# A hybrid decoder block on one core: three quarters of the down-projection with seven block products instead of eight

## The chip, the core and the metric

The kernel runs on one core of a Trainium2 chip. The metric is device time in microseconds (us) of one execution. TensorE (PE in the profile) multiplies matrices, VectorE (DVE), ScalarE (ACT) and GpSimd (POOL) work elementwise, and SyncE (SP) issues every DMA of this kernel from one queue, in order. Each engine executes its instructions in the order in which they stand in its program and waits on semaphores for the others.

## The reference, cut to what matters

The block has two token mixers in parallel (a Mamba-2 scan and a gated DeltaNet), merges them, and ends with a squared-ReLU MLP. The change touches the part behind the mixers:

```python
merged = jax.nn.sigmoid(gate_ssm) * y_ssm + jax.nn.sigmoid(gate_gdn) * y_gdn
x = x + g1 * rmsnorm(merged @ w_out[l], norm_mix_post[l])

h = rmsnorm(x, norm_mlp_pre[l]) * (1.0 + sc2) + sh2
y = jnp.square(jax.nn.relu(h @ w_mlp_up[l])) @ w_mlp_down[l]
x = x + g2 * rmsnorm(y, norm_mlp_post[l])
```

There are 512 tokens, a model width of 1024 and 4096 hidden units, all in float32.

## The kernel before, in words

**Precision.** Every large product is made of three matmuls on rounded operands. A float32 operand is split into a rounded high part and a low remainder: ACT casts it (`whi`, line 145), DVE subtracts (`wlo`, line 146). The helper `mm3` (lines 150 to 152) then issues high times high, low times high, high times low. The third matmul is the one that needs the weight's low half. `dense_w` (lines 140 to 147) loads a 512 KB weight tile into `raw` (three buffers), and splits it into `whi` and `wlo` (three buffers each).

**Stages around the change.** After the mixers come the two up-projections of the branches (lines 1240 to 1267), the output projection `w_out` (lines 1333 to 1350), the norms and the residual, and the MLP. The output projection works in two halves of 256 tokens; each half uses eight weight tiles, one for every 12 matmuls. Behind each half follows a chain of small steps (`sums`, `norms`, `chans`), which ends in the transposed input `h2` of the MLP. The rows that gate and scale the residual (`gates`, built from `adr` and from `rows` through the tiles `rb`) and the residual `x1` are asked for ahead of this stage in the code (lines 1272 to 1285). A scheduler of the tile framework settles the order on each queue, so that in the program the loads of `gate` and `x1` lie in the up-projections, and the four loads of `rb` between weight tiles of the output projection.

**The MLP.** It is cut into four quarters of 1024 hidden units. A quarter has eight hidden tiles (24 matmuls of 128x512 each, then ReLU on ACT and the square with its split on ACT and DVE, lines 1363 to 1380), and then the down-projection: for each half of the output columns four weight tiles, each used by 24 matmuls (four groups of 128 tokens, two tiles of 128 hidden units, three matmuls). That makes 192 matmuls of 128x512 for a quarter. The results are added into `ya` (four tiles, lines 1405 to 1410). The last quarter also sums squares and makes the output.

**Order.** In this part nothing is ordered by hand: each engine follows the order that the scheduler chose when the program was built, and a tile's buffer is reused when its last reader is done. A load into a reused buffer thus waits in the SP queue for the engine that read the buffer last, and everything behind it in that queue waits too.

## Time and profile before

| | |
|---|---|
| median of three timed runs | 1484.27 us (1483.4 to 1485.38) |
| profiled execution: its own time | 1484.77 us |
| profiled execution: span of its instructions | 1483.1 us |
| PE busy | 1458.1 us (98% of the span) |
| DVE, ACT, POOL busy | 862.5, 732.6, 370.2 us |
| granted TensorE clock, mean | 0.996 |
| output projection starts on PE | at 1068.2 us |
| first hidden tile finished | at 1134.8 us |
| one quarter of the MLP | 88.1 us |

The span runs from the first to the last instruction; the execution's own time lies 1.7 us above it. A row of a timeline gives the start, the duration, the engine, the line, the operation with output and inputs, and in brackets how long the engine had been idle and who ended that. Matmuls overlap in their pipeline: one of 128x512 is listed with 0.39 us, but the next one starts some 0.23 us after it, and it is this distance that counts. A row of a table by windows gives the busy time of each engine in that stretch, then the granted clock (1.00 is full speed), the share of the DMA engines that was busy, and GB/s.

### The profile page before, as it was taken

Reading aid. Unit: us, or ns where it says so; the run is one execution under the profiler, and the core shown is the slowest. Engines: PE = TensorE matmul, PEld = TensorE weight load, DVE = VectorE, ACT = ScalarE, POOL = GpSimd, SP = SyncE. Lnnn points to the kernel's source line nnn. Section 1 sums busy time; section 2 is a strip of 40 time slices with the busy share of each in tenths; the row PEclk is TensorE's granted clock in tenths of the full one; section 3 lists DMA queues with packets and bytes.
Section 4 is the critical chain, followed back from the end, with each engine's and each line's share of the span. In section 5 each row is a group of like instructions: output and inputs, shape, how many; then the busy total and the mean of one; then the engine's idle time right before and its main releaser. Section 6 shows DMA issues by size and latency. Waiting matters only on the chain. (4 is left out here: it accounts for less than half of the span.)

```text
span 1483.1 us, 22692 instructions
## 1 busy us (share of the span) xinstructions
PE 1458.1 (98%) x8592; PEld 1241.0 (84%) x8592; DVE 862.5 (58%) x1522; ACT 732.6 (49%) x1379; POOL 370.2 (25%) x691
## 2 busy tenths in 40 slices
PE   9999999999999999999999899999999999999998
PEld 7788898879989889888888788888878888888886
DVE  3565577677767777676777634444477324343444
ACT  6575545673764747645665635333355333132232
POOL 3005444341814607336623410000011000000002
PEclk9999999999999999999999999999999999999999
DMA  9323434543434524344343449543372233223221
GB/s 360 127 97 118 150 103 125 128 137 97 151 119 138 158 81 151 121 116 138 116 137 119 158 170 331 175 156 127 110 239 88 97 100 100 89 96 99 93 95 69
DMA packets 87070, 199.47 MB, mean 134 GB/s; under 512 B 32504, under 2 KB 33024, under 8 KB 86960
## 3 DMA queue, kind: packets, MB, share of 16 engines
q1 hardware_dynamic: 86960, 198.01, 41.3%
q8 instruction: 68, 1.11, 0.3%
q14 instruction: 42, 0.34, 0.1%
HBM read 181.10 MB, written 16.88 MB: 133 GB/s over the span
## 5 line engine op out<-in xcount | busy, mean ns | idle before, releaser
L150 PE MATMUL ps<-hT,whi 128*128 128x512 f32 x688 | 285.7, 415 | 4.8 <-ACT whi L469 4.3
L151 PE MATMUL ps<-hT,wlo 128*128 128x512 f32 x688 | 269.8, 392 | 1.2 <-DVE wlo L471 1.2
L152 PE MATMUL ps<-hT,whi 128*128 128x512 f32 x688 | 269.9, 392 | 0.0
L146 DVE TENSOR_TENSOR wlo<-raw,whi 128x1024 fp32r<-128x1024 f32 x114 | 140.0, 1229 | 199.7 <-ACT whi L145 199.7
L145 ACT CAST whi<-raw 128x1024 fp32r<-128x1024 f32 x114 | 119.4, 1048 | 210.1 <-PE pl L151 61.9
L150 PE MATMUL ps<-whi,hT 128*128 128x256 f32 (+1 forms) x536 | 166.3, 310 | 2.2 <-ACT y L715 1.4
L471 DVE TENSOR_TENSOR wlo<-raw,whi 128x1024 fp32r<-128x1024 f32 x103 | 128.1, 1244 | 64.2 <-ACT whi L469 60.3
L150 PEld LDWEIGHTS ps<-hT,whi 128*128 128x128 f32 x688 | 129.9, 189 | 31.9 <-ACT whi L469 4.5
L152 PE MATMUL ps<-wlo,hT 128*128 128x256 f32 (+1 forms) x536 | 154.3, 288 | 0.6 <-DVE wlo L471 0.6
L151 PE MATMUL ps<-whi,hT 128*128 128x256 f32 (+1 forms) x536 | 153.8, 287 | 0.0
L152 PEld LDWEIGHTS ps<-hT,whi 128*128 128x128 f32 x688 | 129.7, 189 | 28.3
L151 PEld LDWEIGHTS ps<-hT,wlo 128*128 128x128 f32 x688 | 130.1, 189 | 25.8 <-DVE wlo L471 2.4
L469 ACT CAST whi<-raw 128x1024 fp32r<-128x1024 f32 x103 | 107.3, 1044 | 67.4 <-PE ps L152 47.1
L533 DVE SCALAR_TENSOR_TENSOR cv<-ps,col,cv 128x511 f32<-128x511 f32 (+1 forms) x180 | 133.0, 742 | 8.0 <-ACT cv L527 5.4
L150 PEld LDWEIGHTS ps<-whi,hT 128*128 128x128 f32 x536 | 102.1, 190 | 5.8 <-ACT y L715 1.6
L825 POOL TENSOR_TENSOR tm<-Ub,Nb 128x60 f32<-128x60 f32 (+24 forms) x248 | 93.7, 378 | 52.5 <-DMA Nb<-btd 37.6
L151 PEld LDWEIGHTS ps<-whi,hT 128*128 128x128 f32 x536 | 102.1, 190 | 2.2
L152 PEld LDWEIGHTS ps<-wlo,hT 128*128 128x128 f32 x536 | 101.8, 190 | 2.0 <-DVE wlo L471 0.8
L827 POOL TENSOR_TENSOR Ub<-Ub,tm 128x60 f32<-128x60 f32 (+24 forms) x248 | 95.0, 383 | 19.4
L1416 POOL TENSOR_TENSOR ya<-ya,gate 128x512 f32<-128x512 f32 x4 | 5.8, 1466 | 324.8 <-ACT junk L1414 324.8
L150 PE MATMUL pl<-hT,whi 128*128 128x512 f32 (+1 forms) x184 | 66.6, 363 | 1.0 <-DVE hT L195 1.0
L151 PE MATMUL pl<-hT,wlo 128*128 128x512 f32 (+1 forms) x184 | 66.1, 362 | 0.4 <-DVE wlo L146 0.4
(502 smaller groups left out, 3049.0 us busy)
## 6 DMA issues: line engine op xcount, KB each, us to landing
raw<-in_w_ch SPq DMA_DIRECT2D x81, 512.0 KB
raw<-in_w_ada SPq DMA_DIRECT2D x48, 512.0 KB
raw<-in_w_z SPq DMA_DIRECT2D x32, 512.0 KB
raw<-in_w_up SPq DMA_DIRECT2D x32, 512.0 KB
raw<-in_w_mu SPq DMA_DIRECT2D x32, 512.0 KB
raw<-in_w_md SPq DMA_DIRECT2D x32, 512.0 KB
dc<-acd SPq DMA_DIRECT2D x16, 512.0 KB
ydr<-y SPq DMA_DIRECT2D x32, 256.0 KB
```

Of the source, the lines that this page charges most:

```text
L145: sc.copy(hi, raw)
L146: ve.tensor_sub(out=lo, in0=raw, in1=hi.bitcast(F32))
L150: pe.matmul(ps, lhsT=lhs[0], rhs=rhs[0], start=first, stop=False)
L151: pe.matmul(ps, lhsT=lhs[1], rhs=rhs[0], start=False, stop=False)
L152: pe.matmul(ps, lhsT=lhs[0], rhs=rhs[1], start=False, stop=last)
L469: sc.copy(hi, raw)
L471: ve.tensor_sub(out=lo, in0=raw, in1=hi.bitcast(F32))
L533: ve.scalar_tensor_tensor(out=t[:, s:], in0=ps[:, :T - s], scalar=col[:, o + k:o + k + 1], in1=t[:, s:], op0=MUL, op1=ADD)
L825: gp.tensor_tensor(out=t3, in0=Ub[:, 0:r, j:j + 1].to_broadcast([P, r, n]), in1=Nb[:, j:j + 1, j + 1:32].to_broadcast([P, r, n]), op=MUL)
L827: gp.tensor_tensor(out=Ub[:, 0:r, j + 1:32], in0=Ub[:, 0:r, j + 1:32], in1=t3, op=SUB)
L1416: gp.tensor_tensor(out=y, in0=y, in1=gates[1][:, hs], op=MUL)
```

## The change

**Seven products.** In quarters 0, 1 and 2 the down-projection of a quarter is seen as a product of two-by-two blocks: tokens in halves of 256, hidden units in the even and the odd tiles of 128, output columns in halves of 512. The new function `down7` forms sums of activation blocks and sums of weight blocks, makes seven products of blocks instead of eight, and adds the products into `ya`. It runs in four groups (the calls of `stage`, which the text below calls groups 1 to 4): groups 1, 2 and 3 have two block products each, group 4 has one. A block product is 24 matmuls of 128x512, so a quarter has 168 instead of 192. In each group the work goes over four steps `kp`, and each step uses one new pair of `whi` and `wlo`: for two blocks (1024 columns) in groups 1 to 3, for one (512 columns) in group 4.

**Who makes the sums.** All block sums are made on POOL: per step three subtractions of weight blocks of 128x512 (`tt` and `wr`, lines 1415 to 1417), one more in place while group 1 is split (line 1454), and four sums of activation blocks of 128x256 (`s12` and `pr`, lines 1425, 1426, 1427, 1430). The split of the summed blocks goes as before, a cast on ACT and a subtraction, the latter on DVE in groups 1 and 3 and for the weights of group 2, and on POOL for the activations of group 2 and for all of group 4 (line 1386 is the line of every such subtraction). The weights of such a quarter are loaded straight into eight buffers `wr`, all eight of which a quarter uses; those with the first half of the columns are last read on DVE in group 3, those with the second half are last read on POOL in group 4.

**Reads of running sums.** The bank pair `pa` gathers products over three groups and is read after each; it is the first to be finished in the last step of a group, and its reads are issued right then (`read`).

**Memory.** To make room, four tables of the mixers move to a pool that is closed earlier, and the tiles of the norms (`gate0`, `x1`, `xn`) live in a pool that closes before the MLP. So `x1` is written to DRAM (`x1d`, four stores of 512 KB) and read back before the last quarter, and the loads of `gate0`, the `rb` tiles and `x1` move into a function `residual`, called inside the first half of the output projection.

```diff
+    x1d = dram.tile([NC, P, D], F32, name="x1d")
+    gate1 = fin.tile([P, D], F32, name="gate1")
...
+    def residual():
+        for n, g in enumerate((gate0, gate1)):
+            nc.sync.dma_start(out=g, in_=adr[n].partition_broadcast(P))
+            for r, fn in ((n, ve.tensor_add), (2 + n, ve.tensor_mul)):
+                bb = lp.tile([P, D], F32, tag="ob", name="rb", bufs=2)
+                nc.sync.dma_start(out=bb, in_=rows[r].partition_broadcast(P))
+                fn(out=g, in0=g, in1=bb)
+        for t in range(NC):
+            xx = lp.tile([P, D], F32, name=f"x1{t}")
+            nc.sync.dma_start(out=xx, in_=x[t * P:(t + 1) * P, :])
+            x1.append(xx)
...
+            nc.sync.dma_start(out=x1d[t], in_=x1[t])
...
+                if not half and not hf and kp == 2:
+                    residual()
...
+    def halves(src, dst, en):
+        sc.copy(dst[0], src)
+        en.tensor_tensor(out=dst[1], in0=src, in1=dst[0].bitcast(F32), op=SUB)
+        return dst
+
+    def unit(src, n, en):
+
+        u = mp.tile([P, 2, n, 256], F32R, tag="act", name="unit", bufs=8)
+        return halves(src, (u[:, 0], u[:, 1]), en)
+
+    def wide(src, en=None):
+
+        n = src.shape[1]
+        return halves(src, [wp.tile([P, 2, T], F32R, tag=tag, name=tag)[:, 0:n] for tag in ("whi", "wlo")], en or ve)
+
+    def product(ps, u, ub, w, wb, tt, first, last):
+        ts = slice(tt * P, (tt + 1) * P)
+        for n, (i, j) in enumerate(((0, 0), (1, 0), (0, 1))):
+            pe.matmul(ps, lhsT=u[i][:, ub, ts], rhs=w[j][:, wb], start=first and n == 0, stop=last and n == 2,
+                      skip_group_check=True)
+
+    def down7(q):
+
+
+        raw, tb, pr, s12, u1 = {}, [], [], [], []
+        for kp in range(4):
+            for hf in range(2):
+                raw[hf, kp] = mp.tile([P, 2, T], F32, tag="wr", name="wr", bufs=8)
+                nc.sync.dma_start(out=raw[hf, kp].rearrange("p a b -> p (a b)"), in_=w_md[q, hf, kp])
+            b1, b2 = raw[0, kp], raw[1, kp]
+            t = mp.tile([P, 2, T], F32, tag="tt", name="tt", bufs=4)
+            gp.tensor_tensor(out=t[:, 0], in0=b2[:, 0], in1=b1[:, 0], op=SUB)
+            gp.tensor_tensor(out=t[:, 1], in0=b2[:, 1], in1=t[:, 0], op=SUB)
+            gp.tensor_tensor(out=b2[:, 0], in0=b2[:, 1], in1=b2[:, 0], op=SUB)
...
+            sm = mp.tile([P, 2, 256], F32, tag="s12", name="s12", bufs=4)
+            gp.tensor_tensor(out=sm[:, 0], in0=a[:, 1], in1=a[:, 3], op=ADD)
+            gp.tensor_tensor(out=sm[:, 1], in0=sm[:, 0], in1=a[:, 0], op=SUB)
+            gp.tensor_tensor(out=a[:, 1], in0=a[:, 0], in1=a[:, 1], op=SUB)
+            s12.append(sm)
+            u1.append(unit(a[:, 0:4:2], 2, ve))
+            gp.tensor_tensor(out=a[:, 2], in0=a[:, 2], in1=sm[:, 1], op=SUB)
...
+        def stage(us, ws, plan, read=None):
+
+            for kp in range(4):
+                w = ws(kp)
+                u = us(kp)
+                for n, (ps, ub, wb, start) in enumerate(plan if kp < 3 else plan[::-1]):
+                    for tt in range(2):
+                        product(ps[tt], u, ub, w, wb, tt, start and kp == 0, kp == 3)
+                        if kp == 3 and n == 0 and read:
+                            read(tt)
...
+        def w1(kp):
+            w = wide(raw[0, kp])
+            gp.tensor_tensor(out=raw[0, kp][:, 1], in0=raw[0, kp][:, 1], in1=tb[kp][:, 1], op=SUB)
+            return w
...
+        stage(lambda kp: u1[kp], w1, [(pc, 1, 1, True), (pa, 0, 0, True)], lambda tt: add(tt, 0, pa[tt], True))
...
+        stage(lambda kp: unit(s12[kp], 2, gp), lambda kp: wide(tb[kp]), [(pb_, 0, 0, True), (pa, 1, 1, False)],
+              lambda tt: add(tt, 1, pa[tt], True))
...
+        stage(lambda kp: unit(pr[kp][:, 1:4:2], 2, ve), w3, [(pc, 1, 0, True), (pa, 0, 1, False)], third)
...
+        stage(lambda kp: unit(pr[kp][:, 2:3], 1, gp), lambda kp: wide(raw[1, kp][:, 1:2], gp), [(pb_, 0, 0, False)])
...
+    for q in range(3):
+        down7(q)
```

**Where instructions move.** The first place is the SP queue in the output projection. The first row is behind the first seven of the sixteen weight tiles in both programs; rows with a minus stood there before, rows with a plus stand there now (x with a number is a residual tile, gate_10839 the gate of the first residual).

```order
-L1278 DMA rb<-in_rows 128x1024 x2
-L142 DMA raw<-in_w_out 128x1024 x2
-L1278 DMA rb<-in_rows 128x1024 x2
+L1280 DMA gate_10839<-adr 128x1024
+L1283 DMA rb<-in_rows 128x1024 x2
+L1287 DMA x_10928<-in_x 128x1024
+L1283 DMA rb<-in_rows 128x1024
+L1287 DMA x_10930<-in_x 128x1024
+L1283 DMA rb<-in_rows 128x1024
+L1287 DMA x_10932<-in_x 128x1024
+L1287 DMA x_10934<-in_x 128x1024
 L142 DMA raw<-in_w_out 128x1024 x7
```

The eighth weight tile stood behind two loads of `rb`; it now stands behind nine loads of 512 KB each.

The second place is POOL around the end of a quarter's down-projection. Before, POOL had nothing to do from the norms to the last quarter; these rows stood next to each other (`s1` belongs to the norms, `ya` to the last quarter):

```order
L1324 TENSOR_TENSOR s1_11277<-s1_11277,mhalf_78 128x1
L1324 TENSOR_TENSOR s1_11282<-s1_11282,mhalf_78 128x1
L1416 TENSOR_TENSOR ya0_11508<-ya0_11508,gate1_10845 128x512
L1416 TENSOR_TENSOR ya1_11509<-ya1_11509,gate1_10845 128x512
L1416 TENSOR_TENSOR ya2_11510<-ya2_11510,gate1_10845 128x512
```

Now these twelve stand there at the end of quarter 0. The rows of line 1386 belong to quarter 0: `unit` is an activation operand and `wlo_12023`, `wlo_12036`, `wlo_12049`, `wlo_12062` are the weights' low halves of the four steps of group 4. The rows of lines 1415 to 1417 make the weight sums of quarter 1 from its freshly loaded tiles `wr_12076` and on.

```order
L1415 TENSOR_TENSOR tt_12080<-wr_12078,wr_12076 128x512 [waits DMAHW2_49,DMAHW1_49,DVE_49]
L1386 TENSOR_TENSOR unit_12065<-pr_11695,unit_12065 128x256 [waits PE_49,Activation_49]
L1416 TENSOR_TENSOR tt_12080<-wr_12078,tt_12080 128x512 [waits Pool_49]
L1417 TENSOR_TENSOR wr_12078<-wr_12078 128x512 [waits DVE_49]
L1386 TENSOR_TENSOR wlo_12023<-wr_11527,whi_12022 128x512 [waits PE_49,Activation_49]
L1415 TENSOR_TENSOR tt_12165<-wr_12163,wr_12161 128x512 [waits DMAHW4_49,DMAHW3_49]
L1416 TENSOR_TENSOR tt_12165<-wr_12163,tt_12165 128x512 [waits Pool_49]
L1417 TENSOR_TENSOR wr_12163<-wr_12163 128x512 [waits DVE_49]
L1386 TENSOR_TENSOR wlo_12036<-wr_11550,whi_12035 128x512 [waits PE_49,Activation_49]
L1386 TENSOR_TENSOR wlo_12049<-wr_11604,whi_12048 128x512 [waits DVE_49,PE_49,Activation_49]
L1415 TENSOR_TENSOR tt_12250<-wr_12248,wr_12246 128x512 [waits DMAHW6_49,DMAHW5_49]
L1386 TENSOR_TENSOR wlo_12062<-wr_11689,whi_12061 128x512 [waits PE_49,Activation_49]
```

Seven subtractions for the next quarter stand between the operands of group 4. At the end of quarter 1 the same seven stand between them; at the end of quarter 2 none does.

The third place is the SP queue for the loads of quarter 1's weights (the first four of eight go into buffers that DVE frees in group 3):

```order
L1412 DMA wr_12161<-in_w_md 128x1024 [waits DMAHW3_49,DVE_49]
L1412 DMA wr_12163<-in_w_md 128x1024 [waits DVE_49]
L1412 DMA wr_12246<-in_w_md 128x1024 [waits Pool_49]
L1412 DMA wr_12248<-in_w_md 128x1024 [waits DMAHW6_49,Pool_49]
L1412 DMA wr_12331<-in_w_md 128x1024 [waits DMAHW7_49,Pool_49]
L1412 DMA wr_12333<-in_w_md 128x1024 [waits DMAHW0_49,DVE_49,Pool_49]
```

Before, these weights went through the three `raw` buffers; now the fifth to eighth load wait for POOL, that is for the four rows of `wlo` above, one after the other.

## The prediction

> **What bounds the kernel now.** I read the busy shares first, then the table by windows over the stages that the change touches.

> ```profile
> PE 1458.1 (98%) x8592; PEld 1241.0 (84%) x8592; DVE 862.5 (58%) x1522; ACT 732.6 (49%) x1379; POOL 370.2 (25%) x691
> ...
> core 0: us, PE busy (x) PEld busy (x) DVE busy (x) ACT busy (x) POOL busy (x), PEclk, DMA share, GB/s
> 1074.00:1090.00 16.00, 16.00 (x72) 13.23 (x72) 10.76 (x9) 6.29 (x10) 0.00 (x0) 1.00 0.89 303
> 1254.00:1342.00 88.00, 88.00 (x385) 72.10 (x384) 35.30 (x40) 24.91 (x32) 0.00 (x0) 1.00 0.29 96
> ```

> PE sets the time. In a quarter of the MLP (88 us) it never waits, while POOL does nothing and DVE and ACT stand idle more than half the time. In the output projection PE doesn't wait either, but there the DMA engines are 89% busy. So every matmul taken out of the MLP is worth its full distance to the next one, and every wait that reaches PE costs its full length.

> What a matmul costs is read from the timeline of ACT, at points where ACT waits for PE once per 24 matmuls: the first two rows lie in the hidden tiles, the last two in the down-projection.

> ```profile
> 1222.19 0.60 ACT L1375 ACTIVATE rl<-pl 128x512 f32<-128x512 f32 x1 [3.38 <-PE pl L152]
> 1227.63 0.60 ACT L1375 ACTIVATE rl<-pl 128x512 f32<-128x512 f32 x1 [3.38 <-PE pl L152]
> ...
> 1177.60 1.05 ACT L145 CAST whi<-raw 128x1024 fp32r<-128x1024 f32 x1 [4.52 <-PE pl L151]
> 1183.18 1.05 ACT L145 CAST whi<-raw 128x1024 fp32r<-128x1024 f32 x1 [4.53 <-PE pl L151]
> ```

> 5.44 us for 24 (0.227 each) in the hidden tiles, 5.58 us for 24 (0.2325 each) in the down-projection.

> **The matmuls.** Three quarters lose 24 matmuls each: 72 x 0.2325 = 16.7 us (16.3 if the new ones ran at the pace of the hidden tiles). A quarter's groups 1 to 3 last 48 matmuls, 11.15 us each, group 4 lasts 5.6 us.

> **The work of the other engines.** Prices: ACT cast of 1024 columns 1.05 us (above); the others from the groups by form.

> ```profile
> L146 DVE TENSOR_TENSOR wlo<-raw,whi 128x1024 fp32r<-128x1024 f32 x53 | 65.1, 1228 | 101.7 <-ACT whi L145 101.7
> L1410 DVE TENSOR_TENSOR ya<-pl,ya 128x512 f32<-128x512 f32 x14 | 9.5, 688 | 3.1 <-PE pl L152 2.8
> L1408 ACT COPY ya<-pl 128x512 f32<-128x512 f32 x5 | 2.9, 587 | 2.8 <-PE pl L152 2.8
> L1416 POOL TENSOR_TENSOR ya<-ya,gate 128x512 f32<-128x512 f32 x4 | 5.8, 1466 | 324.8 <-ACT junk L1414 324.8
> L1318 POOL TENSOR_TENSOR x<-xn,x 128x512 f32<-128x512 f32 x4 | 5.9, 1479 | 1.8 <-DVE xn L1313 1.7
> L1080 POOL TENSOR_TENSOR xk<-xk,dsk 128x512 f32<-128x512 f32 x16 | 19.5, 1219 | 0.0
> L1156 POOL TENSOR_TENSOR xk<-xk,zs 128x256 f32<-128x256 f32 x32 | 27.4, 865 | 0.0
> ```

> Per quarter DVE gets 16 subtractions of 1024 columns, 16 of 512 and up to 16 adds: 16 x 1.23 + 32 x 0.69 = 41.7 us of 82.6. ACT comes to about the same. POOL gets 24 of 512 columns and 20 of 256: 24 x 1.47 + 20 x 0.87 = 52.7 us of 82.6. All three have room over the quarter. In groups 1 to 3 a step takes PE 2.8 us against 2.3 us for a cast and a subtraction, with three buffers: covered. So DVE and ACT are costed at nothing, and so is POOL wherever it only has to be done on average. The edge is group 2 of quarter 0: POOL can begin only when the second hidden tile is squared, at about 1140 on the clock of before (the first is done at 1134.8), and has 16 operations of 512 columns and 16 of 256 until the first operand of group 2 is there: 37.4 us, to 1177.4. Group 2 starts after five more hidden tiles and group 1, at 1140 + 5 x 5.44 + 11.15 = 1178.4. So 1 us is to spare and I take nothing; at 1.7 us per operation PE would wait 2.7 us.

> **Group 4: POOL on PE's path.** Here order, not load, decides. POOL's row `wlo_12036` (step 1 of group 4) stands behind six weight sums of the next quarter, and `wlo_12062` (step 3) behind a seventh. That one reads `wr_12248`, which is loaded into the buffer that `wlo_12036` has just read. So inside group 4 there is a chain: POOL subtracts, SP issues a load, POOL waits for its landing, adds, subtracts, PE goes on. The landing of a lone 512 KB load has its price in the first two rows: issued at 1105.49, waited for until 1108.95, so 3.5 us.

> ```profile
> 1105.49 6.12 SPq L142 DMA_DIRECT2D raw<-in_w_mu  x4
> ...
> 1108.95 1.05 ACT L145 CAST whi<-raw 128x1024 fp32r<-128x1024 f32 x1 [1.70 <-DMA raw<-in_w_mu]
> ```

> Count from the end of group 2 (time 0); group 3 ends at 11.15, and group 4 ideally at 16.7. `wr_12078` goes into a buffer that DVE frees just before time 0 (second step of group 3's split), so the first of the twelve rows starts at about 2.3. From it to the end of `wlo_12036` are eight operations of 512 columns and one of 256; then 3.5 us for the load (`wlo_12049` lies beside it), two more operations, and 1.0 us for the four matmuls behind the low half. With p for one operation of 512 columns the group ends at 2.3 + 8p + 0.87 + 3.5 + 2p + 1.0 = 7.7 + 10p. That is 10p - 9.0 us late. In quarter 1 the same rows start at 2.6 with the 256 one behind them: 10p - 9.6. In quarter 2 nothing stands between, and POOL is in time.

> p: the two rows with two full operands (lines 1416 and 1318 of the kernel before) say 1.47. I take that: 5.7 + 5.1 = 10.8 us. Ends: 1.22 (line 1080, whose second operand is repeated over columns) gives 5.8 us; 1.81, the longest of the four of line 1416 below, 17.6 us. A gain is excluded: PE can't run ahead of these operands.

> ```profile
> L1416 POOL TENSOR_TENSOR ya<-ya,gate x4: 1289/1380/1812, 1451.4 to 1456.8; 128x512 f32<-128x512 f32 x4
> ```

> [...]

> **The burst of loads.** The rows of the SP queue, of a step of the gate on DVE, of the eighth weight tile on ACT and PE, and the best rate of the DMA engines (in the prologue):

> ```profile
> 1065.97 7.59 SPq L142 DMA_DIRECT2D raw<-in_w_out  x3
> 1073.88 0.80 SPq L1278 DMA_DIRECT2D rb<-in_rows  x2
> 1075.95 3.01 SPq L142 DMA_DIRECT2D raw<-in_w_out  x2
> ...
> 1081.48 1.23 DVE L1279 TENSOR_TENSOR gate<-gate,rb 128x1024 f32<-128x1024 f32 x1 [1.41 <-DMA rb<-in_rows]
> ...
> 1082.59 1.05 ACT L145 CAST whi<-raw 128x1024 fp32r<-128x1024 f32 x1 [1.82 <-DMA raw<-in_w_out]
> ...
> 1087.20 0.39 PE L150 MATMUL pl<-whi,hT 128*128 128x512 f32 x1
> ...
> 24.00:28.00 4.00, 4.00 (x32) 1.00 1.03 410
> ```

> Before, the eighth weight tile is asked for at 1075.95, lands at 1082.5 and is used at 1087.2. Behind the seventh tile nine loads of 0.524 MB now stand first, from 1073.9 on: with the tile itself 5.24 MB. The landing of the lone load above is 2.2 us of lead and 1.3 us of transfer. At 410 GB/s the tile lands at 1073.9 + 2.2 + 12.8 = 1088.9; at the 303 GB/s of this stage, where rows are spread over all partitions, at 1093.4. Half of the ten are such spread rows, so I take 1091.2. SP's own waits (two `rb` buffers, freed by DVE) end earlier. Cast, subtraction and hand-overs take 2.5 us, of which two matmuls run ahead of the low half: PE goes on at 1093.2 in effect, **6.0 us** late (3.8 to 8.3). Nothing gives it back: the chains of the norms start from the end of this half. The stores and re-reads of `x1` (eight loads' worth, where the DMA engines are 29% busy or PE is three weights ahead) cost nothing; without that cover, 1.3 us each.

> **The clock.** PE's gap there is some 5 us, and in group 4's last step 3.6 us (`wlo_12049` is there at 2.3 + 0.87 + 9p = 16.4, six matmuls later it is 17.8, and `wlo_12062` comes at 21.4). What a gap does shows in the trace once, and at the end:

> ```profile
> 832.47 0.28 PE L152 MATMUL ps<-wlo,hT 128*128 128x256 f32 x1
> 837.02 0.79 PE L150 MATMUL ps<-hT,whi 128*128 128x512 f32 x1 [4.27 <-ACT whi L469]
> ...
> 840.15 0.63 PE L152 MATMUL ps<-hT,whi 128*128 128x512 f32 x1
> 840.58 0.63 PE L150 MATMUL ps<-hT,whi 128*128 128x512 f32 x1
> ...
> 836.00:838.00 2.00, 0.79 (x1) 0.67 0.24 60
> 842.00:844.00 2.00, 2.00 (x9) 0.62 0.25 33
> ...
> 1475.00:1476.00 1.00, 0.88 (x8) 1.00 0.95 354
> 1478.00:1479.00 1.00, 0.00 (x0) 0.70 0.00 0
> ```

> The clock halved 4 us after the last matmul (832.75 to 836.7) in the one place, 2.5 us after (1475.9 to 1478.4) in the other, and came back at 843.5, 6.5 us after PE went on; matmuls lay 0.43 us apart. So a fall costs half of 6.5: 3.2 us. The burst's gap is long enough: 3.2. For the two of group 4 I take one fall: 3.2 (none to 6.5).

> **The sum**, on the profiled execution: 1484.8 - 16.7 + 10.8 + 6.0 + 3.2 + 3.2 = 1491.3. The median of the runs lies 0.5 us below that execution: **1491 us**, 0.4% slower.

> **The rivals.**

> *POOL keeps up (the other side).* If p is near 1.2, group 4 is 5.8 us late and its gaps stay too short for the clock: 1484.8 - 16.7 + 5.8 + 9.2 = 1483.1, no change. It decides at 20p - 18.6 = 7.5, p = 1.3; below 1.17 it is faster by over 3 us. For it: the 16 operations of line 1080 took 1.22, with DVE busy. Against: they have a repeated operand, and both rows without one lie at 1.47. [...]

> *The burst lands in time.* At 410 GB/s PE waits 3.8 us and the clock stays: 1484.8 - 16.7 + 10.8 + 3.8 + 3.2 = 1485.9, so 1485. For it: the rate was reached when 512 KB weights streamed. Against: 0.89 of the engines' time gave only 303 in this very stage.

> *The saving arrives.* Both together: 1484.8 - 16.7 + 5.8 + 3.8 = 1477.7; if no operand is late at all, 1468. The saving itself is certain, PE being busy throughout.

> *POOL and DVE slow each other.* The new subtractions read two operands on both engines at the same time. Rows for it, after the first norm:

> ```profile
> 1095.74 3.01 POOL L1318 TENSOR_TENSOR x<-xn,x 128x512 f32<-128x512 f32 x2 [0.87 <-DVE xn L1313]
> 1098.17 1.66 DVE L146 TENSOR_TENSOR wlo<-raw,whi 128x1024 fp32r<-128x1024 f32 x1
> ```

> DVE's subtraction took 1.66 instead of 1.23 where POOL was adding. With p = 1.81, two falls in group 4 and the slow burst: 1484.8 - 16.7 + 17.6 + 6.5 + 8.3 + 3.2 = 1503.7. Against: POOL's pair there took 1.5 each with DVE busy throughout, so 1.47 has most of it in it. [...]

> **How the numbers follow.** Forecast 40%, POOL keeps up 18%, burst in time 15%, saving arrives 17%, contention 10%. A measurement of this kernel can tell some 0.2% (3 us) from no change. Faster by more: 17% of the saving and 6% of POOL keeping up, 23%. Slower by more: 38% of the forecast, 3% of the burst, 10% of contention, 51%. The rest, 26%, is the same. The forecast's own range is 1486 to 1497. The range that holds 8 in 10 goes from 1475, which leaves out half of the saving's case, to 1501, which leaves out most of contention's.

> **What would show it.** Right: the eighth weight tile's cast waits for its load until about 1091, PE stands for some 5 us there and the clock reads 0.5 for a few us after; POOL's rows of line 1386 with 512 columns at the ends of quarters 0 and 1 are the last releaser of PE, with a wait for the load of `wr` in front of the last, and quarter 2 has none. Quarters then take about 88, 88 and 82.6 us before the clock. Wrong: PE shows no wait over 2 us between 1087 and the last quarter; or POOL's operations take 1.2; or waits come up where I cost nothing, on DVE and ACT in groups 1 to 3, on the first operand of group 2 in quarter 0, or on a bank of PSUM that a running sum's read holds.

## The result, and the profile after

The changed kernel takes **1500.66 us** (median of four runs, 1500.24 to 1501.95) against 1484.83 us of the kernel before, measured beside it: ratio 1.0107, 95% interval 1.0094 to 1.0119. It is 15.8 us slower. The forecast was 1491 us, slower by 6.2: the right side and inside the wide range (1475 to 1501), but outside its own range of 1486 to 1497 and less than half of the size. The profiled execution has a span of 1498.8 us, 15.7 more than before.

The first line of the page, and the waits of PE from 1040 us on (engine, tile and line; what was waited for; us in total, how often, the longest):

```profile
PE 1453.5 (97%) x8520; PEld 1232.5 (82%) x8520; DVE 906.6 (60%) x1546; ACT 776.3 (52%) x1463; POOL 541.2 (36%) x823
...
PE pl L1402 <- POOL wlo L1386: 9.0, 4, 3.0
PE pl L150 <- ACT whi L145: 7.9, 1, 7.9
PE pl L1402 <- POOL unit L1386: 3.2, 1, 3.2
PE pl L1402 <- DVE wlo L1386: 1.3, 2, 0.6
```

72 matmuls are gone, but PE's busy time fell by only 4.6 us, and its idle time rose from 25.0 to 45.3. The first two waits are those that the forecast names: group 4 on POOL, and the eighth weight tile of the output projection. The third stands where the forecast had costed nothing.

To see which stretch of the program lost how much, I use the first hidden tile of each quarter, as ACT reads it, and the load of three `w_out` tiles ahead of the burst. In the changed kernel:

```profile
1065.71 7.59 SPq L142 DMA_DIRECT2D raw<-in_w_out  x3
...
1144.09 0.60 ACT L1381 ACTIVATE rl<-pl 128x512 f32<-128x512 f32 x1 [1.60 <-PE pl L152]
1234.07 0.60 ACT L1381 ACTIVATE rl<-pl 128x512 f32<-128x512 f32 x1 [5.39 <-PE pl L152]
1324.93 0.60 ACT L1381 ACTIVATE rl<-pl 128x512 f32<-128x512 f32 x1 [4.61 <-PE pl L152]
1408.89 0.60 ACT L1381 ACTIVATE rl<-pl 128x512 f32<-128x512 f32 x1 [4.58 <-PE pl L152]
```

The differences between such rows are the lengths of the stages. The same rows of every profile of this study give this table (us). The time at which the first of these rows comes differs by up to 5.7 us between the profiles, though the code ahead of it is the same, so stages tell more than spans. In each row of the table, "loads to first hidden tile" is the stage ahead of the MLP, and "the rest" is the last quarter with the output.

| kernel | loads to first hidden tile | quarter 0 | quarter 1 | quarter 2 | the rest |
|---|---|---|---|---|---|
| before | 68.8 | 82.0 | 88.2 | 88.2 | 90.0 |
| the change | 78.4 | 90.0 | 90.9 | 84.0 | 89.9 |
| the change, second profile | 78.8 | 90.5 | 90.0 | 84.0 | 90.0 |
| the change, third profile | 77.6 | 87.7 | 93.0 | 83.9 | 89.9 |
| group 4 on DVE | 77.4 | 82.5 | 84.7 | 83.6 | 90.0 |
| loads split | 70.6 | 90.0 | 90.5 | 84.1 | 89.9 |
| before, burst alone | 81.3 | 82.0 | 88.2 | 88.2 | 89.9 |
| gaps filled | 77.7 | 90.4 | 91.4 | 84.0 | 90.0 |
| groups 2 and 4 on DVE | 80.4 | 80.3 | 85.3 | 85.3 | 89.9 |
| groups 2 and 4, loads split | 70.0 | 81.3 | 85.7 | 85.2 | 90.0 |
| sums shared | 79.0 | 85.6 | 91.8 | 83.9 | 89.9 |
| four `rb` buffers | 76.5 | 88.1 | 91.7 | 84.0 | 89.9 |
| loads split, group 4 on DVE | 69.9 | 82.1 | 84.7 | 83.5 | 90.0 |
| these two and sums shared | 70.1 | 78.6 | 84.7 | 83.5 | 90.0 |

A quarter without 24 matmuls should be 5.6 us shorter than before: 76.4, 82.6, 82.6. Measured by that the change is late by 9.6 us before the MLP and by 13.6, 8.3 and 1.4 us in the quarters, 32.9 in all; less the 16.7 saved, that is the 15.7 of the span, within 0.5.

The table also shows how far single profiles scatter. Six of them have the same code ahead of the MLP (the change three times, group 4 on DVE, groups 2 and 4 on DVE, sums shared), and that stage takes 77.4 to 80.4 us in them, with a wait for the eighth weight tile of 6.6 to 9.5 us. Quarter 0 of the change takes 87.7 to 90.5 us, quarter 1 takes 90.0 to 93.0.

**The burst.** SP's loads, the cast of the eighth weight tile on ACT, and the matmul that waits for it:

```profile
1073.61 0.33 SPq L1280 DMA_DIRECT2D gate<-adr  x1
...
1074.96 0.51 SPq L1287 DMA_DIRECT2D x<-in_x  x1
1080.78 0.33 SPq L1283 DMA_DIRECT2D rb<-in_rows  x1
...
1084.78 2.18 SPq L142 DMA_DIRECT2D raw<-in_w_out  x3
...
1093.89 1.04 ACT L145 CAST whi<-raw 128x1024 fp32r<-128x1024 f32 x1 [13.39 <-DMA raw<-in_w_out]
...
1094.99 0.79 PE L150 MATMUL pl<-whi,hT 128*128 128x512 f32 x1 [7.90 <-ACT whi L145]
```

The wait is there, but the tile is issued only at 1084.78: SP itself stood still between 1075.5 and 1080.8, since the third `rb` load needs a buffer that DVE had not yet freed. The forecast held that this wait ends earlier than the engines have moved the data.

**Group 4 of quarter 0.** POOL's rows, and the two matmuls that wait for them:

```profile
1208.60 1.30 POOL L1415 TENSOR_TENSOR tt<-wr 128x512 f32<-128x512 f32 x1 [5.45 <-DMA wr<-in_w_md]
...
1218.14 2.49 POOL L1386 TENSOR_TENSOR wlo<-wr,whi 128x512 fp32r<-128x512 f32 x2
1222.80 1.83 POOL L1415 TENSOR_TENSOR tt<-wr 128x512 f32<-128x512 f32 x1 [2.16 <-DMA wr<-in_w_md]
1224.59 1.26 POOL L1386 TENSOR_TENSOR wlo<-wr,whi 128x512 fp32r<-128x512 f32 x1
...
1219.46 0.80 PE L1402 MATMUL pl<-wlo,unit 128*128 128x512 f32 x1 [3.02 <-POOL wlo L1386]
...
1225.91 0.80 PE L1402 MATMUL pl<-wlo,unit 128*128 128x512 f32 x1 [2.11 <-POOL wlo L1386]
```

This is the chain of the forecast, link by link: weight sums, a subtraction, a load into the buffer just read, its landing, a sum, a subtraction, PE.

**Group 2 of quarter 0.** POOL's first sum of the quarter, the subtraction that PE needs, and PE:

```profile
1148.23 1.19 POOL L1425 TENSOR_TENSOR s<-pr 128x256 f32<-128x256 f32 x1 [11.65 <-ACT pr L1422]
...
1188.89 3.40 POOL L1386 TENSOR_TENSOR unit<-s,unit 128x512 fp32r<-128x512 f32 x2
...
1190.65 0.50 PE L1402 MATMUL pl<-whi,unit 128*128 128x512 f32 x1 [3.19 <-POOL unit L1386]
```

From the first sum to the operand POOL took 42.4 us without a pause; the forecast had 37.4.

### The profile page after: what moved, and what is told of

Its sections match the earlier page's. It is cut to its first block, busy times and chain, and to the rows that moved or that the text cites. A ratio compares the mean times of both kernels' runs of the same rounds, so it can differ in the third digit from the quotient of the medians.

```text
span 1498.8 us, 22883 instructions
## 1 busy us (share of the span) xinstructions
PE 1453.5 (97%) x8520; PEld 1232.5 (82%) x8520; DVE 906.6 (60%) x1546; ACT 776.3 (52%) x1463; POOL 541.2 (36%) x823
## 5 line engine op out<-in xcount | busy, mean ns | idle before, releaser
L150 PE MATMUL ps<-hT,whi 128*128 128x512 f32 x688 | 285.6, 415 | 4.8 <-ACT whi L469 4.3
L151 PE MATMUL ps<-hT,wlo 128*128 128x512 f32 x688 | 269.9, 392 | 1.2 <-DVE wlo L471 1.2
L152 PE MATMUL ps<-hT,whi 128*128 128x512 f32 x688 | 270.0, 392 | 0.0
L146 DVE TENSOR_TENSOR wlo<-raw,whi 128x1024 fp32r<-128x1024 f32 x90 | 115.3, 1282 | 174.5 <-ACT whi L145 174.4
L150 PE MATMUL ps<-whi,hT 128*128 128x256 f32 (+1 forms) x536 | 166.3, 310 | 2.2 <-ACT y L715 1.4
L145 ACT CAST whi<-raw 128x1024 fp32r<-128x1024 f32 x90 | 94.4, 1049 | 140.7 <-PE pl L152 43.9
L471 DVE TENSOR_TENSOR wlo<-raw,whi 128x1024 fp32r<-128x1024 f32 x103 | 128.2, 1245 | 64.4 <-ACT whi L469 62.1
L150 PEld LDWEIGHTS ps<-hT,whi 128*128 128x128 f32 x688 | 129.9, 189 | 32.0 <-ACT whi L469 4.5
L152 PE MATMUL ps<-wlo,hT 128*128 128x256 f32 (+1 forms) x536 | 154.2, 288 | 0.3 <-DVE wlo L471 0.3
L151 PE MATMUL ps<-whi,hT 128*128 128x256 f32 (+1 forms) x536 | 153.8, 287 | 0.0
L152 PEld LDWEIGHTS ps<-hT,whi 128*128 128x128 f32 x688 | 129.7, 188 | 28.3
L151 PEld LDWEIGHTS ps<-hT,wlo 128*128 128x128 f32 x688 | 130.1, 189 | 25.8 <-DVE wlo L471 2.3
L469 ACT CAST whi<-raw 128x1024 fp32r<-128x1024 f32 x103 | 107.3, 1044 | 68.5 <-PE ps L152 47.1
L150 PEld LDWEIGHTS ps<-whi,hT 128*128 128x128 f32 x536 | 102.1, 190 | 5.7 <-ACT y L715 1.6
L151 PEld LDWEIGHTS ps<-whi,hT 128*128 128x128 f32 x536 | 102.1, 190 | 2.2
L152 PEld LDWEIGHTS ps<-wlo,hT 128*128 128x128 f32 x536 | 101.9, 190 | 1.7 <-DVE wlo L471 0.5
L827 POOL TENSOR_TENSOR Ub<-Ub,tm 128x60 f32<-128x60 f32 (+24 forms) x248 | 91.6, 369 | 19.4
L1402 PE MATMUL pl<-whi,unit 128*128 128x512 f32 x240 | 78.1, 407 | 3.6 <-POOL unit L1386 3.2
L784 POOL TENSOR_SCALAR_AFFINE_SELECT dec<-dec 128x1024 f32<-128x1024 f32 x8 | 9.0, 1122 | 164.4 <-DVE dec L779 136.5
```

The costliest lines, as they stand in the source:

```text
L145: sc.copy(hi, raw)
L146: ve.tensor_sub(out=lo, in0=raw, in1=hi.bitcast(F32))
L150: pe.matmul(ps, lhsT=lhs[0], rhs=rhs[0], start=first, stop=False)
L151: pe.matmul(ps, lhsT=lhs[1], rhs=rhs[0], start=False, stop=False)
L152: pe.matmul(ps, lhsT=lhs[0], rhs=rhs[1], start=False, stop=last)
L469: sc.copy(hi, raw)
```

## The experiments

**Group 4 on DVE.** The order on POOL against DVE coming as late.

```diff
-        stage(lambda kp: unit(pr[kp][:, 2:3], 1, gp), lambda kp: wide(raw[1, kp][:, 1:2], gp), [(pb_, 0, 0, False)])
+        stage(lambda kp: unit(pr[kp][:, 2:3], 1, ve), lambda kp: wide(raw[1, kp][:, 1:2]), [(pb_, 0, 0, False)])
```

> Edit: the changed kernel, with the subtractions of group 4 (weights and activations) on DVE instead of POOL. Theory (order on POOL makes group 4 late, and PE's halved clock behind each gap adds to it): the three or four gaps of PE in group 4, 9.0 us in all, go, and with them the falls of the clock behind them, about 14 us at half clock, 6 to 7 us; the kernel takes 1485 to 1486 us. The 3.2 us before an operand of group 2 in quarter 0 stay. Rival 1 (POOL is only the last of several: DVE, which holds the adds of the running sums, comes as late): at most 3 us are won, 1497 or more. Rival 2 (the halved clock has another cause than these gaps): the 9 us go, the clock stays low as long as now, 1491 to 1492 us.

Measured: 1486.31 us, ratio to before 1.0020 (1.0009 to 1.0032), 14.3 us less than the change (13.3 when each is measured against the kernel before beside it). PE's waits in the MLP:

```profile
PE pl L1402 <- POOL unit L1386: 3.2, 1, 3.2
PE pl L1402 <- DVE wlo L1386: 1.9, 3, 0.6
```

No wait of group 4 is left, and quarters 0 and 1 are 7.5 and 6.2 us shorter: group 4 on POOL costs **13.7 us**, more than its 9.0 us of waits. The rest lay in PE's busy time, at half clock: in the change the granted clock reads 0.50 for two stretches of 3.4 us at the end of quarter 0 (from 1218.89 and from 1225.71) and for one of 6.8 us at the end of quarter 1 (from 1311.04).

**Loads split.** Five loads instead of nine ahead of the eighth tile.

```diff
                 if not half and not hf and kp == 2:
-                    residual()
+                    gate(0, gate0)
+                if not half and hf and kp == 2:
+                    residual((0, 1))
+                if half and not hf and kp == 2:
+                    residual((2, 3))
...
     norms(1)
+    gate(1, gate1)
```

> Edit: the changed kernel, with the nine loads of the residual split: the rows for gate0 and two tiles of x1 (five loads) where they were, two tiles of x1 and the three loads for gate1 later, between weight tiles of the second half. Theory (the burst makes the eighth weight tile late): four loads of 0.524 MB less, at some 320 GB/s 6.5 us; PE's wait of 7.9 us falls to about 1.4, the fall of the clock behind it (2.4 us) goes: 1491 to 1493 us. Rival (the wait is set by something else than the number of loads ahead, or the loads moved back are late in their turn at the norms): 1498 or more, with a wait of over 4 us at the eighth tile or a new one behind the norms.

Measured: 1491.80 us, ratio 1.0055 (1.0042 to 1.0068). The stage before the MLP falls from 78.4 to 70.6 us; the longest wait in it is 1.0 us, and 1.8 us of the burst's 9.6 are left. The theory holds.

**Before, with the burst alone.**

```diff
+                if not half and not hf and kp == 2:
+                    residual()
```

with the loads of the gates and `x1` of the kernel before taken out of their old place.

> Edit: the kernel before, with nothing changed but the loads of gate0, gate1 and x1, which are issued by the function of the changed kernel at its place in the first half of the output projection; the MLP is the old one. Theory (burst and clock): PE waits 7.9 us for the eighth weight tile, the clock falls behind that (2.4 us), and the wait of 1.2 us of before at the twelfth tile goes: 9 us slower, 1493 to 1494 us. My forecast's term was 6.0 + 3.2 = 9.2, so this run doesn't tell it from the theory but from the rival that the burst lands in time (3.8 us, no fall: 1488 to 1489 us).

Measured: 1496.42 us, ratio 1.0088 (1.0073 to 1.0103), 12.6 us slower. The MLP's stages are those of before to 0.1 us; the stage ahead of them is 12.5 us longer. In the three profiles of the change it is 8.8 to 10.0 us longer. The waits:

```profile
PE pl L150 <- ACT whi L145: 9.1, 1, 9.1
PE pl L192 <- ACT hf L194: 2.0, 1, 2.0
```

So the burst alone makes the old kernel slower, and "lands in time" is out. It is not quite the same burst: in this build the load of `gate1`, which the change issues at 910 us, stands in it too, so that ten loads and not nine lie ahead of the eighth tile, and the transposes wait 2.0 us on ACT instead of 0.6. How much of the 3 us more comes from that stays open, since the same code of the change is 11.6 us longer than before in one of its six profiles (the run with groups 2 and 4 on DVE).

**Gaps filled.** Is the halved clock a loss of its own?

```diff
+            if fill and n == fill[0]:
+                for _ in range(fill[1]):
+                    pe.matmul(fill[2], lhsT=u[0][:, ub, ts], rhs=w[0][:, wb], start=True, stop=True,
+                              skip_group_check=True)
...
+                if not half and hf and kp == 3:
+                    idle = dpsum()
+                    for _ in range(28):
+                        pe.matmul(idle, lhsT=mg[kp][0][:, 0:P], rhs=w[0][:, 0:T], start=True, stop=True)
```

> Edit: the changed kernel, with matmuls whose result nobody reads put into the gaps of PE: 28 ahead of the first matmul of the eighth weight tile of the output projection (6.4 of 7.9 us), 10 and 7 ahead of the third matmul of steps 1 and 3 of group 4 in quarters 0 and 1 (2.3 and 1.6 us). The data that PE waits for come no earlier. Theory (each gap of 2 us or more is followed by some 3.5 to 5 us at half the clock): the falls at these places go, and 6 to 8 us are won although work is added: 1493 to 1495 us. Rival (the halved clock isn't tied to the gaps, or costs nothing since PE then catches up): no change or up to 1.5 us slower, 1500 to 1502 us.

Measured: 1504.24 us, ratio 1.0140 (1.0125 to 1.0155). The theory falls: nothing was won. By the medians 3.6 us were lost; between the two profiles it is 2.8, of which 2.4 lie ahead of the output projection, where the code is the same. Without these it is the rival's result, and of its two reasons the second: PE catches up. The clock did stay up right behind the burst and in quarter 1 (in quarter 0 it fell once in group 4, at 1228.0), but look at what PE met next:

```profile
1097.40 0.50 PE L150 MATMUL pl<-whi,hT 128*128 128x512 f32 x1 [1.56 <-ACT whi L145]
1108.17 0.50 PE L152 MATMUL pl<-wlo,hT 128*128 128x512 f32 x1 [1.05 <-DVE wlo L146]
...
1320.95 0.50 PE L1410 MATMUL pl<-wlo,unit 128*128 128x512 f32 x1 [2.27 <-POOL wlo L1390]
```

At full clock PE reached the eleventh tile sooner and waited 1.05 us for its low half, and in quarter 1 it waited 2.27 us for POOL's second `wlo` instead of 0.95. The three stages take 77.7, 90.4 and 91.4 us, 259.5 in all, against 258.3 to 259.3 in the three profiles of the change; 6 to 8 less had been expected. So half clock between two waits on the same late chain cost next to nothing here: the slower PE arrived when the operand did. My accounting of the trace before this run, waits plus time lost at half clock, was a true account of PE but not of what could be won.

**Groups 2 and 4 on DVE.** The wait ahead of group 2: is it the subtraction on POOL, or the sums?

```diff
-        stage(lambda kp: unit(s12[kp], 2, gp), lambda kp: wide(tb[kp]), [(pb_, 0, 0, True), (pa, 1, 1, False)],
+        stage(lambda kp: unit(s12[kp], 2, ve), lambda kp: wide(tb[kp]), [(pb_, 0, 0, True), (pa, 1, 1, False)],
```

beside the edit for group 4.

> Edit: as the run with group 4's subtractions on DVE, and the activations of group 2 on DVE too, so that POOL only makes sums. Theory (POOL's backlog in quarter 0 makes the first operand of group 2 late, since its subtraction stands behind the sums): the wait of 3.2 us and the half clock behind it (1.7 to 2.7 us) go, quarter 0 takes 77 instead of 82.5 us, the kernel 1480 to 1482 us. Rival (the sums themselves are late, or DVE, with 1.9 us of subtractions and adds per step of 2.8 us, becomes late in group 2): quarter 0 takes 80 us or more, 1484 or more.

Measured: 1488.66 us, ratio 1.0031 (1.0018 to 1.0043), no better than with group 4 alone. (It is 2.3 us more, but the profile has 3.0 more ahead of the MLP, where the code is the same; the three quarters take 250.9 against 250.8.) The rival holds, in both of its halves. ACT, and then the matmuls of group 2 in quarter 0:

```profile
1187.02 0.62 ACT L1385 CAST unit<-s 128x512 fp32r<-128x512 f32 x1 [4.99 <-POOL s L1426]
...
1190.97 0.50 PE L1402 MATMUL pl<-wlo,unit 128*128 128x512 f32 x1 [1.59 <-DVE wlo L1386]
...
1275.94 0.50 PE L1402 MATMUL pl<-wlo,unit 128*128 128x512 f32 x1 [0.94 <-DVE wlo L1386]
```

ACT, in order, waited 5 us for the last of POOL's sums before it could cast group 2's weights; and in quarter 1 (1275.94), where POOL has no backlog, DVE is late. The same edits with the loads split gave

> Edit: all subtractions on DVE as in the run above, and the loads of the residual spread as in the run with split loads. If the three parts add up (14.3 us for group 4, 8.9 for the loads, some 5 for group 2, all from 1500.7): 1472 to 1474 us, 0.7% faster than the kernel before; the 72 matmuls less (16.7 us) would then have been won in full but for some 4 to 5 us. Rival (the parts share a limit, or DVE takes over as the last releaser in groups 2 and 4): 1478 us or more.

Measured: 1479.35 us, ratio 0.9965 (0.9953 to 0.9977). Faster than before, but 5 to 7 us above what adding up the parts promised, since the part on group 2 was no gain: quarter 2, with nothing else to lose, takes 85.2 us instead of 84.0.

**Sums shared.** POOL's backlog itself.

```diff
+            en = ve if q == 0 and kp > 1 else gp
-            gp.tensor_tensor(out=t[:, 0], in0=b2[:, 0], in1=b1[:, 0], op=SUB)
-            gp.tensor_tensor(out=t[:, 1], in0=b2[:, 1], in1=t[:, 0], op=SUB)
-            gp.tensor_tensor(out=b2[:, 0], in0=b2[:, 1], in1=b2[:, 0], op=SUB)
+            en.tensor_tensor(out=t[:, 0], in0=b2[:, 0], in1=b1[:, 0], op=SUB)
+            en.tensor_tensor(out=t[:, 1], in0=b2[:, 1], in1=t[:, 0], op=SUB)
+            en.tensor_tensor(out=b2[:, 0], in0=b2[:, 1], in1=b2[:, 0], op=SUB)
```

> Edit: the changed kernel; only the three weight sums of steps 2 and 3 of quarter 0 (six subtractions of 512 columns) are made on DVE instead of POOL, in the hidden tiles, where DVE is idle more than half the time. The activations of group 2 stay on POOL. Theory (the wait ahead of group 2 comes from POOL's backlog of sums, not from the engine that makes the last subtraction): POOL is 6 x 1.3 to 1.5 = 8 to 9 us earlier, the wait of 3.2 us and the half clock behind it (up to 1.7) go, quarter 0 takes 85 to 87 us instead of 88 to 90, the kernel 1496 to 1498 us. Rival (something else, ACT's casts or the loads, holds group 2 too): no more than 1 us is won, 1499.5 or more.

Measured: 1496.98 us, ratio 1.0083 (1.0066 to 1.0099), 3 to 4 us less than the change (1500.66, and 1500.22 in its second series). The wait on `unit` is gone, and quarter 0 takes 85.6 us instead of 87.7 to 90.5, although PE now waits 1.1 us for DVE in the hidden tiles, where DVE makes the sums. The backlog was the cause.

**Four `rb` buffers.** Did SP's own waits set the burst?

```diff
-                bb = lp.tile([P, D], F32, tag="ob", name="rb", bufs=2)
+                bb = lp.tile([P, D], F32, tag="ob", name="rb", bufs=4)
```

> Edit: the changed kernel with four buffers for the rows rb instead of two, so that SP doesn't wait for DVE within the burst. My forecast held that SP's waits end earlier than the engines have moved the data; in the changed kernel the weight tile is issued at 1084.8, 11 us after the first load of the burst. Theory of bandwidth: the tile is issued some 6 us earlier but lands no earlier, since nine loads go first at 300 to 330 GB/s: within 1 us of 1500.5. Rival (SP's waits set it): the tile lands 3 us or more earlier, 1494 to 1497 us.

Measured: 1498.72 us, ratio 1.0089 (1.0072 to 1.0106); the intervals of this and of the change overlap. By the profile the answer lies between the two. SP's row, the wait, and the DMA engines from the first load of the burst on (share of time busy and GB/s are the last two numbers):

```profile
1076.39 15.41 SPq L142 DMA_DIRECT2D raw<-in_w_out  x5
...
1088.96 0.80 PE L150 MATMUL pl<-whi,hT 128*128 128x512 f32 x1 [5.18 <-ACT whi L145]
...
1070.30:1087.30 17.00, 13.48 (x60) 10.84 (x58) 8.43 (x7) 4.06 (x7) 0.00 (x0) 1.00 0.98 365
```

Issued 6 us after the first load instead of 11, the tile still makes PE wait 5.2 us, with the engines busy 98% of the time. So some 5 us of the wait are what the engines need to move the data. What is left for SP is 2 to 2.7 us by the three profiles of the change (7.3 to 7.9), and 1.4 to 4.3 by all six with this code; the medians do not show it.

**All that helps.** First the loads split and group 4 on DVE, then the sums shared as well; the diffs are those above.

> Edit: the loads of the residual split and group 4's subtractions on DVE, group 2 as in the changed kernel. If the two parts add up: 1500.5 - 14.3 - 8.9 = 1477.3; 1476 to 1479 us. Rival (they share a limit): 1481 or more.

Measured: 1478.66 us, ratio 0.9951 (0.9936 to 0.9966). The parts add up.

> Edit: the loads of the residual split, group 4's subtractions on DVE, and the weight sums of steps 2 and 3 of quarter 0 on DVE, the activations of group 2 on POOL. Theory (three separate causes: group 4 14.3, loads 8.9, backlog of quarter 0 3.2 to 4.9): 1472 to 1474.5 us, the fastest so far. Rival (DVE, now with more work in quarter 0, becomes late, or quarters 1 and 2 keep what they lose): 1477 or more.

Measured: 1476.31 us, ratio 0.9940 (0.9923 to 0.9957), 0.6% faster than the kernel before and the fastest of all; 2 us above what I expected. PE's longest waits after 1040 us:

```profile
PE pl L1408 <- DVE wlo L1392: 2.5, 4, 0.6
PE ps L151 <- DVE wlo L146: 1.3, 1, 1.3
```

**The change twice more.** Does a gap's length decide whether the clock falls?

> The changed kernel itself, unchanged, for a second profile and its times beside the other runs. Theory (the clock is decided on a grid of 3.41 us that runs free of the program: a period in which PE is busy less than about half is followed by a period at half the clock, one over 0.6 is not): the gaps of PE are the same within 0.5 us, but the grid lies elsewhere, so that other gaps are followed by half clock or other lengths of it; all edges lie a whole number of 3.41 us apart; the time stays within 1499 to 1503 us. Rival (the length of a gap decides): the same falls behind the same gaps.

> The changed kernel once more, for a third profile: as for the second, another place of the grid, the same gaps, another set of falls. Rival: the same falls behind the same gaps in all three.

Measured: 1500.22 us (ratio 1.0110, 1.0093 to 1.0128) and, in a single run, 1500.81. The large gaps stand at the same six places in all three profiles, though not to the 0.5 us that I had expected: in group 4 they shift against each other (in quarter 1, 2.95 and 0.95; 2.67 and 1.26; 2.67 and 2.95). Which of them is followed by half clock differs. Here are periods of 3.41 us at the end of quarter 0, first of the change's first profile, then of its second. In each row the first pair of numbers is the period's length and PE's busy time, and the granted clock is the third number from the end.

```profile
1215.47:1218.89 3.42, 0.97 (x5) 0.46 (x3) 0.00 (x0) 0.62 (x1) 3.34 (x4) 1.00 0.40 144
1218.89:1222.30 3.41, 2.84 (x7) 2.29 (x8) 0.03 (x1) 1.04 (x1) 1.75 (x2) 0.50 0.55 168
1222.30:1225.71 3.41, 1.50 (x7) 0.88 (x5) 1.19 (x1) 1.05 (x1) 2.91 (x2) 1.00 0.42 139
1225.71:1229.13 3.42, 3.22 (x8) 2.58 (x9) 2.39 (x2) 1.04 (x1) 2.61 (x3) 0.50 0.64 210
```

```profile
1216.82:1220.24 3.42, 1.61 (x7) 1.35 (x8) 0.00 (x0) 0.58 (x1) 3.00 (x3) 1.00 0.19 43
1220.24:1223.65 3.41, 1.45 (x7) 0.82 (x5) 1.23 (x1) 1.52 (x2) 1.75 (x2) 1.00 0.76 261
1223.65:1227.07 3.42, 2.63 (x6) 2.15 (x7) 1.80 (x2) 0.90 (x1) 3.21 (x3) 0.50 0.45 144
1227.07:1230.48 3.41, 3.41 (x9) 2.64 (x9) 3.41 (x3) 0.14 (x1) 2.28 (x2) 0.50 0.86 304
```

In the first profile the gap of 3.0 us (up to 1219.46) lies mostly in one period, which PE fills to 28%, and the next one is at half clock. In the second a gap of 2.8 us (up to 1218.62) is split by the edge at 1216.82; its larger part lies in a period filled to 47%, and the clock stays. In the first profile even the gap of 2.1 us (up to 1225.91) is followed by half clock, since it lies in a period filled to 44%. The rival, that the length decides, is out. Quarters 0 and 1 together take 180.8, 180.5 and 180.7 us in the three profiles, whichever falls they have, which agrees with the run with filled gaps.

## Why the prediction was wrong in size

**The 72 matmuls, 16.7 us: right to 1.4.** In the best version (the run with three parts) quarters 0 to 2 take 246.8 us against 258.3, 11.5 less, with 3.8 us of waits on DVE in them; the other 1.4 us show in no wait.

**Group 4, 10.8 us and one fall of 3.2, together 14.0: right, 13.7 measured**, but by errors that cancel. The operation of 512 columns took 1.28 us in the chain, not 1.47, where DVE was idle beside it or read PSUM (one row beside a weight split on DVE took 1.83). By the forecast's own condition (p below 1.3) POOL should then have kept up. The prediction's own line of four such rows begins at 1289 ns; the 1.47 is a mean over rows of two kinds. A p below 1.17, to which the forecast gave 6%, shows in no row of the change's profile: the shortest of POOL's 76 operations of 512 columns behind 1140 us took 1.26. POOL did not keep up, because the chain began 5.3 us after the end of group 2 in quarter 0 and 5.7 in quarter 1, not 2.3 and 2.6. In quarter 0 half of that is DVE, which freed the buffer late, so that the load was issued 0.5 us after the end of group 2 where the forecast's 2.3 needs 1.2 us before it. The other half is its landing: three loads were issued within 3 us and shared the engines (busy 70% of the time from 1202.0 to 1208.6, at 229 GB/s), and the one that POOL needed, the second, landed 4.8 us after its issue instead of 3.5:

```profile
1202.00 0.33 SPq L1412 DMA_DIRECT2D wr<-in_w_md  x1
...
1203.76 0.33 SPq L1412 DMA_DIRECT2D wr<-in_w_md  x1
...
1204.93 0.33 SPq L1412 DMA_DIRECT2D wr<-in_w_md  x1
```

The last four matmuls took 2.1 us instead of 1.0, at a granted clock of 0.50.

**The burst, 6.0 us and one fall of 3.2, together 9.2: right, 9.6 measured** (8.8 to 10.0 in three profiles), but again by errors that cancel. PE waited 7.9 us and not 6.0; a wait of 1.2 us at the twelfth tile of the kernel before went away in return; and the fall of the clock, by the run with filled gaps, was worth little by itself. The sentence that SP's waits end earlier was wrong by some 2 us.

**Group 2 of quarter 0, costed at nothing: this step failed.** The margin of 1 us was worked out from 1.47 and 0.87 us for one operation, taken where POOL and DVE seldom meet. POOL began 1 us earlier behind the first hidden tile than I took, which left 1.8 us to spare, but it took 5.0 us longer. Here are the three groups of its rows that were slowest, over the quarter's sums:

```profile
L1454 POOL TENSOR_TENSOR wr<-wr,tt 128x512 f32<-128x512 f32 x4 | 8.1, 2030 | 0.0
L1386 POOL TENSOR_TENSOR unit<-s,unit 128x512 fp32r<-128x512 f32 x3 | 5.1, 1727 | 0.0
L1427 POOL TENSOR_TENSOR pr<-pr 128x256 f32<-128x256 f32 x4 | 4.9, 1233 | 0.0
```

2.03 and 1.73 instead of 1.47, 1.23 instead of 0.87, at the time when DVE made its subtractions in the hidden tiles and in group 1. Over all 32 operations up to the first operand, the 16 of 512 columns took 1.59 us on the mean and the 16 of 256 took 1.09, so most of the 5.0 us lies in the short ones. The forecast had this as its last rival and put it at the wrong place: it struck here, not in group 4. It set the rival aside with two rows of POOL of 1.5 us each beside a busy DVE; they took 1.30 and 1.69, and beside the first one DVE was mostly reading PSUM. It cost 3.2 us of waiting and 1.7 at half clock, 4.9 together. In the two runs that take it away quarter 0 is 3.5 and 4.4 us shorter, each with a new wait on DVE of 1.3 and 1.1 us.

**DVE in groups 1 to 3, costed at nothing: this failed too, by 1.7 us that the trace shows.** Group 4 and the backlog leave 4.7 of the 23.3 us of the quarters (1.2, 2.1 and 1.4). In the change PE waits for DVE 0.8 us in quarter 1, 0.8 in quarter 2 and not at all in quarter 0. The other 3.0 us show in no wait on DVE, and their cause stays open. The comparison of 2.3 us of work with 2.8 us a step left out the four reads of running sums, which stand in one piece ahead of a split, and that DVE's operations took longer as well. DVE in quarter 1:

```profile
1280.64 2.94 DVE L1386 TENSOR_TENSOR unit<-pr,unit 128x512 fp32r<-128x512 f32 x2
1283.50 2.47 DVE L1437 TENSOR_TENSOR ya<-pl,ya 128x512 f32<-128x512 f32 x4
1285.89 3.44 DVE L1386 TENSOR_TENSOR wlo<-tt,whi 128x1024 fp32r<-128x1024 f32 x2
```

The two subtractions of 512 columns took 1.47 us on the mean, 0.69 in the forecast's prices. The one of 1024 that PE waited for stood behind them and the four reads; it took its usual 1.21 us itself (the second of the pair took 2.31). PE waited 0.63 us for it, and as long in quarter 2.

So of the 9.2 us that the forecast was short, 4.9 are group 2 and 4.7 are what else the quarters lost, of which 1.7 can be seen as waits on DVE; the others cancel to within 0.5. What can be seen of both is the same omission: prices taken where the two engines seldom met, for a stage in which POOL and DVE work on two full operands at the same time.

**The clock.** The rule I read from two places ("halved 2.5 to 4 us after the last matmul, back after 6.5") was an accident of where the periods of 3.41 us lay. The two falls of 3.2 us in the sum are luck: by the run with filled gaps they were worth little by themselves, and they filled up two terms whose other parts were too small.

## What to carry to other kernels

The saving of 1.1% on the bound engine (16.7 us) was lost here at operands that came late (15.8 us slower in the end), so cost each engine's order at the edges of a stage, not its load over the stage, and price an operation beside the work that will run at the same time (2.03 us and not 1.47 for POOL's slowest group). Time lost at half clock was no loss here where something later in the same chain was late anyway (the three stages took 259.5 us with the gaps filled, 258.3 to 259.3 without); fill a gap and see before you count it. Where a change fails, test its parts one by one: three small edits (a split of loads, another engine for the subtractions of group 4, six sums moved) turned 1.1% slower into 0.6% faster.

## What the runs showed of the hardware that I had not expected

**POOL and DVE took longer beside each other, on the mean by up to a factor of two.** An operation of 512 columns on two full operands took 1.26 to 1.30 us on POOL alone and 2.03 on the mean beside DVE's subtractions of group 1; on DVE 0.69 and 1.47. No run was made to separate this from other causes, but the traces of all 14 profiles leave little room. Behind 1140 us, 251 of POOL's operations of 512 columns ran while DVE did nothing, in 1.25 to 1.30 us each, and 76 ran beside DVE operations that read PSUM, in 1.29 us on the mean. All 301 rows that took over 1.47 us lay beside a DVE operation with two operands in SBUF.
